# Two transformer blocks on one core: attention heads laid out as 96 rows, another input queue, shared norm banks, block-wise evacuation, another order at the end

## The chip, the core and the metric

The kernel runs on one core of a Trainium2 chip. TensorE (PE) multiplies matrices into PSUM banks, VectorE (DVE), ScalarE (ACT) and GpSimd (POOL) do the element-wise work, and transfers are started from a queue of an engine, most of them from SyncE (SP). The metric is the device time of one execution in microseconds (us), lower is better. It is given as the median of several executions; the profile comes from one more.

## What is computed

256 tokens of width 1024 go through two blocks. The parts that the change touches, from the reference:

```python
def first_block(...):
    xn = rmsnorm(x, norm_mix_g[l])
    proj = jnp.einsum('bsd,de->bse', xn, w_in[l])
    q_lat, kv_lat, k_rope, dq, dk, dv, gate_pre = jnp.split(proj, split_idx, axis=-1)
    q = jnp.einsum('bsr,re->bse', rmsnorm(q_lat, mla_q_norm_g[l]), mla_w_uq[l])
    q_nope, q_pe = q[..., :MLA_NOPE_DIM], apply_rope(q[..., MLA_NOPE_DIM:], ...)   # 64 and 32 of 96
    ...
    q_mla = jnp.concatenate([q_nope, q_pe], axis=-1)
    k_mla = jnp.concatenate([k_nope, jnp.broadcast_to(k_pe, (B, S, MLA_HEADS, MLA_ROPE_DIM))], axis=-1)
    o_mla = causal_attention(q_mla, k_mla, v_mla)                                  # 8 heads
    o_diff = rmsnorm(o1 - lam * o2, diff_subln_g[l]) * (1.0 - lambda_init)         # 4 heads, two maps each
    merged = g_mla * (o_mla @ w_branch_mla[l]) + g_diff * (o_diff @ w_branch_diff[l])
    x = x + jnp.einsum('bsd,de->bse', merged, w_out[l])
    hn = rmsnorm(x, norm_ffn_g[l])
    x = x + (silu(hn @ w_ffn_gate[l]) * (hn @ w_ffn_up[l])) @ w_ffn_down[l]

def second_block(...):      # after a norm of its own
    hx = modulate(rmsnorm_2(x, norm1_g[layer]), sh1, sc1)
    x = x + g1 * (jnp.concatenate([pool_x, attn_x], axis=-1) @ w_out[layer])
    h2 = modulate(rmsnorm_2(x, norm2_g[layer]), sh2, sc2)
    x = x + g2 * peer(h2, ...)        # scores over 128 x 128 experts, then u and v of 16384 x 1024
    return rmsnorm_2(x, final_g)
```

## The kernel before

All of it is one launch on one core. Activations lie transposed (features on the 128 partitions, the 256 tokens along the free axis). Weights are f32 and streamed: `Weights` (L138) loads 128x2048 pieces (`raw`, three buffers) by SP's queue, and splits each 128x1024 half into a rounded high part `whi` by ACT (L133) and a rest `wlo` by DVE (L130), three buffers of each. `mm3` (L167) makes one product out of three matmuls, high x high (L171), low x high (L172) and high x low (L173), so each step of a layer needs whi, wlo and the input's halves. `lin_t` (L175) computes output blocks of 128 features, two of them (`grp=2`) in one PSUM bank, and then calls an evacuation function. PSUM has eight banks: tags a, b, c and d, two of each.

The order on every engine is made by a scheduler from the program's order, its dependences and hints (`tc.issue_after` puts work behind a given instruction); no order is written out by hand.

Stages, in the order of time: the input xT is loaded (L339) and split to xh and xl (`split_x`), POOL squares it (L359) and PE sums the squares with a column of ones (L253). Then come the input projection, the latent projections, the rotations (`rope`, L439), the attention with latent heads, that with differential heads, the gates, the branch products wbm and wbd, wo, the feed-forward, the second block with its own attention and wo2, the search of experts, and the expert products over u and v (v: L1091).

- Latent heads: queries and keys are kept as `qn` and `kn` (two heads of 64 rows on one 128-row tile) and `qp` (four heads of 32 rows) with one shared rotary key `kp`. `soft` (L501) makes the scores of two heads with two matmuls each, one over the 64 rows and one over the 32, adds the mask by a third (L502), takes the row extreme by DVE (L504), the exponential by ACT, and transposes by PE (L513). `pv` (L520) multiplies with the values.
- Differential heads use the same `soft` with one matmul of 64 rows per map. Then `od` is normalised (four nt's, POOL's power, L573), transposed (L576) and split to `odh` by ACT (L579) and `odl` by DVE (L580). These feed wbd; `omh` and `oml` of the latent heads feed wbm.
- Norms: `SumSq` adds up squares over feature blocks and sums over partitions with PE into two PSUM banks, one for each half of the tokens. `rsqrt_cols` (L208) writes one column at a time (nt, by DVE), then POOL raises to the power -0.5 (ny, L219), and PE spreads it over rows (L267).
- wo's evacuation `put_x1` (L612) and wo2's `put_x3` (L819) take two output blocks at once.
- The end: two blocks of 128 experts are done per accumulator, in the order of the four accumulators `acc` (two token halves by two column halves). Then DVE multiplies with the gate (L1131), adds x (L1132), ACT squares (L1133), DVE multiplies with the gain (L1134), and after the factor from POOL ACT scales one half (L1138) and DVE the other (L1139).

Of the kernel before, what the change touches and what calls it, by code (L numbers as in the profile page):

```python
# [63 lines left out]
def block_kernel(ctx: ExitStack, tc: tile.TileContext, a: dict, out: bass.AP, dbg=None):  # L64
# [74 lines left out]
    class Weights:  # L139
# [68 lines left out]
    def rsqrt_cols(vs, scale, nm="n", eps=None):  # L208

        n = len(vs)  # L210
        y = small.tile([P, n], F32, tag=f"{nm}y{n}", name="ny")
        t = small.tile([P, n], F32, tag=f"{nm}t{n}", name="nt")
        for i, v in enumerate(vs):
            c = slice(i, i + 1)
            if eps is None:
                nc.vector.tensor_scalar(t[:, c], v, scale, EPS, op0=OP.mult, op1=OP.add)
            else:
                nc.vector.scalar_tensor_tensor(t[:, c], v, scale, eps, op0=OP.mult, op1=OP.add)
# [3 lines left out]
    class SumSq:  # L222
# [3 lines left out]
        def __init__(self, K, ps_fn, tail=2, held=False):  # L226
            self.held = [] if held else None
            self.K, self.k, self.ps, self.head = K, 0, [ps_fn() for _ in range(2)], K - tail
            self.first = True
            if self.head > 0:  # L230
                self.acc = adap.tile([P, S], F32, tag="sqa", bufs=2, name="sqa")

        def add(self, src, scale=None, sq=None):
# [11 lines left out]
            if k >= self.head - 1:  # L245
                if self.held is None:
                    self.total(sq, k)
                else:
                    self.held.append((sq, k))

        def total(self, sq, k):
            for tt in range(2):
                nc.tensor.matmul(self.ps[tt][:, 0:1], sq[:, tt * P:(tt + 1) * P], ones[:, 0:1],  # L253
                                 start=self.first, stop=(k == self.K - 1))
            self.first = False

        def done(self):
            for h in self.held or ():
                self.total(*h)
            return [p_[:, 0:1] for p_ in self.ps]  # L260
# [89 lines left out]
    subg = b1a.tile([P, 1], F32, name="subg")  # L350
    nc.scalar.activation(subg, col("sub"), AF.Copy, scale=1.0 - LAMBDA_INIT)
    load_x(0)
# [56 lines left out]
    nc.vector.tensor_copy(posf, posi)  # L409
    identb = b1a.tile([P, P], BF16, name="identb")  # L410
    nc.vector.tensor_copy(identb, ident)
    maskb = b1a.tile([P, P], BF16, name="maskb")
    nc.vector.tensor_copy(maskb, cs1[:, CB["mask"] - NCB])

    def rope_tables(inv, nm):
# [3 lines left out]
        for shift, kind in ((0.0, "s"), (math.pi / 2, "c")):  # L419
            ki = b1s.tile([P, S], I32, tag="ki", bufs=2, name="ki")  # L420
            nc.vector.tensor_scalar(ki, ang, 1.0 / TWO_PI, shift / TWO_PI, op0=OP.mult, op1=OP.add)
            kf = b1s.tile([P, S], F32, tag="kf", bufs=2, name="kf")
# [16 lines left out]
    def rope(x_, n, rt, cc, ss):  # L439
        for j in range(0, n, 2):  # L440
# [6 lines left out]
            nc.vector.tensor_tensor(x_[:, j:j + m], x_[:, j:j + m], t1[:, :m], op=OP.add)  # L447
# [79 lines left out]
    for qb in range(2):  # L527
        o = ps_d()
        z = small.tile([P, 8], F32, tag="az", name="az")
        for h0 in range(4):  # L530
            b0, r0 = 64 * (h0 % 2), 32 * h0
# [20 lines left out]
    for qb in range(2):  # L552
# [19 lines left out]
        yd = rsqrt_cols([ss[:, h:h + 1] for h in range(4)], 1.0 / 128, "d")  # L572
# [36 lines left out]
    ss1 = SumSq(KD, ps_d, held=True)  # L609
# [12 lines left out]
    b2 = pool(st3, "b2")  # L622
    st3c = ExitStack()
# [5 lines left out]
    hs = scaled_split(x1, KD, lambda k: col("ffn", k), acts, "act")  # L629
# [25 lines left out]
    def modulated(src, rb, gs, sh, hi, lo):  # L655
        for k in range(KD):
            t = adap.tile([P, S], F32, tag="mdt", bufs=4, name="mdt")
# [41 lines left out]
    with tc.high_priority():  # L699
# [8 lines left out]
        for i in range(2):  # L708
            c = slice(i, i + 1)
            nc.vector.scalar_tensor_tensor(t[:, c], sg[i], yf[:, c], yf[:, c], op0=OP.mult, op1=OP.mult)  # L710
        y3 = rsqrt_cols([t[:, 0:1], t[:, 1:2]], 1.0 / D, "m")
# [102 lines left out]
    ss3 = SumSq(KD, ps_d, held=True)  # L814

    def put_x3(j, n, ps):
# [454 lines left out]
```

## Time and profile before

| what | us |
|---|---|
| median of three executions | 1413.62 (1412.87 to 1416.95) |
| the profiled execution | 1420.62 |
| its span (first to last instruction on record) | 1418.8 |
| busy in the span: PE, DVE, ACT, POOL | 1375.2, 1013.1, 704.9, 23.8 |

The mean granted clock of PE over the span was 0.984 of full speed. A busy engine is one that has an instruction in flight; for PE, matmuls overlap in the array, so a row's duration is longer than the distance to the next start, and it is the distance that counts. A gap in brackets is idle time of the engine ahead of that row, with what ended it.

### The profile page before, as it was taken

The page shows a single profiled execution, that of the slowest core. Times are in us where ns is not written, and L with a number is a line of the kernel's source. Part 1 is how long each engine was busy: PE and PEld are TensorE (multiplying, and loading weights), DVE is VectorE, ACT ScalarE, POOL GpSimd, SP SyncE. Part 2 cuts the span into 40 slices and gives each one's busy share as a digit, 9 for nine tenths or more (in the row PEclk, how much of TensorE's full clock was granted, in tenths as well). Part 3 has the DMA queues.
Part 4 walks back from the last instruction along what each step waited for, and adds up shares of the span by engine and source line. Part 5 has one row for each costly group of instructions (what it writes and reads, how often), then busy time and mean ns, then how long its engine had stood idle before and what let it go on. Part 6 is the DMA issues. An engine that isn't in the chain of part 4 may idle for free.

```text
span 1418.8 us, 24208 instructions
## 1 busy us (share of the span) xinstructions
PE 1375.2 (97%) x9776; PEld 1270.8 (90%) x9776; DVE 1013.1 (71%) x1749; ACT 704.9 (50%) x1030; POOL 23.8 (2%) x25
## 2 busy tenths in 40 slices
PE   7999999999999999899999999998999999999997
PEld 6967998999999888899999999998888888888885
DVE  6774777998888646699984489876536555566775
ACT  4443654454546555545454456554344454444443
POOL 1000000000000001000000000000000000000000
PEclk9998999999999999999999999999899999999999
DMA  6452456777795632444555578889975555588762
GB/s 239 154 196 82 141 169 234 269 279 267 262 328 191 218 125 72 152 170 158 187 198 180 178 257 311 296 296 321 340 287 197 190 197 199 198 300 289 262 233 86
DMA packets 88448, 308.86 MB, mean 218 GB/s; under 512 B 6416, under 2 KB 39824, under 8 KB 61200
## 3 DMA queue, kind: packets, MB, share of 16 engines
q1 hardware_dynamic: 78544, 279.26, 57.0%
q10 hardware_dynamic: 9792, 28.05, 5.0%
q8 instruction: 76, 1.25, 0.3%
q14 instruction: 36, 0.29, 0.1%
HBM read 281.08 MB, written 26.21 MB: 217 GB/s over the span
## 4 chain that ended last, share of the span: by engine, by line
PE 88%; DVE 5%; DMA 4%; issue 1%; ACT 1%; POOL 0%; SPq 0%; ACTq 0%; POOLq 0%; DVEq 0%
PE acc L1091 24%; PE psa L173 9%; PE psa L171 9%; PE psa L172 9%; PE psc L173 8%; PE psc L171 8%; PE psc L172 8%; DMA aw<-in_ada 2%; PE psb L501 2%; DVE wlo L130 2%; PE psd L1012 1%; PE psb L1012 1%; DMA gh<-ggd 1%; PE psd L771 1%; PE psb L759 1%
## 5 line engine op out<-in xcount | busy, mean ns | idle before, releaser
L133 ACT ACTIVATE whi<-raw 128x1024 fp32r<-128x1024 f32 (+1 forms) x426 | 448.0, 1053 | 502.7 <-PE psa L172 181.6
L130 DVE TENSOR_TENSOR wlo<-raw,whi 128x1024 fp32r<-128x1024 f32 (+1 forms) x426 | 517.4, 1217 | 240.6 <-ACT whi L133 236.9
L171 PE MATMUL psc<-h2h,whi 128*128 128x256 f32 x1024 | 294.3, 288 | 6.4 <-ACT whi L133 6.4
L173 PE MATMUL psc<-h2h,wlo 128*128 128x256 f32 x1024 | 293.8, 288 | 4.2 <-DVE wlo L130 4.2
L172 PE MATMUL psc<-h2l,whi 128*128 128x256 f32 x1024 | 292.7, 286 | 0.0
L171 PEld LDWEIGHTS psc<-h2h,whi 128*128 128x128 f32 x1024 | 199.8, 195 | 7.0 <-ACT whi L133 7.0
L173 PEld LDWEIGHTS psc<-h2h,wlo 128*128 128x128 f32 x1024 | 199.5, 195 | 4.9 <-DVE wlo L130 4.9
L172 PEld LDWEIGHTS psc<-h2l,whi 128*128 128x128 f32 x1024 | 199.8, 195 | 0.0
L1091 PE MATMUL acc<-wlo,wgh 128*128 128x512 f32 x512 | 160.2, 393 | 0.0
L1091 PE MATMUL acc<-whi,wgl 128*128 128x512 f32 x512 | 158.7, 390 | 0.0
L1091 PE MATMUL acc<-whi,wgh 128*128 128x512 f32 x512 | 138.5, 389 | 0.0
L1091 PEld LDWEIGHTS acc<-whi,wgl 128*128 128x128 f32 x512 | 96.1, 188 | 20.2
L1091 PEld LDWEIGHTS acc<-whi,wgh 128*128 128x128 f32 x512 | 96.0, 188 | 20.1
L1091 PEld LDWEIGHTS acc<-wlo,wgh 128*128 128x128 f32 x512 | 94.6, 188 | 19.7
L171 PE MATMUL psa<-acth,whi 128*128 128x256 f32 x352 | 99.9, 284 | 2.0 <-DVE ft L638 1.2
L173 PE MATMUL psa<-acth,wlo 128*128 128x256 f32 x352 | 99.9, 284 | 1.9 <-DVE wlo L130 1.9
L172 PE MATMUL psa<-actl,whi 128*128 128x256 f32 x352 | 99.8, 284 | 0.2 <-DVE actl L293 0.2
L171 PE MATMUL psa<-xh,whi 128*128 128x256 f32 x240 | 71.1, 296 | 8.0 <-ACT whi L133 8.0
L173 PE MATMUL psa<-xh,wlo 128*128 128x256 f32 x240 | 70.4, 293 | 2.6 <-DVE wlo L130 2.6
L172 PE MATMUL psa<-xl,whi 128*128 128x256 f32 x240 | 71.0, 296 | 0.0
L316 DVE SCALAR_TENSOR_TENSOR jk<-aw,row_c 128x1024 bf16<-128x1024 f32 x48 | 58.6, 1220 | 14.8 <-DMA aw<-in_ada 14.4
L171 PEld LDWEIGHTS psa<-acth,whi 128*128 128x128 f32 x352 | 66.9, 190 | 2.6 <-ACT whi L133 1.4
(415 smaller groups left out, 2462.6 us busy)
## 6 DMA issues: line engine op xcount, KB each, us to landing
raw<-in_uT SPq DMA_DIRECT2D x64, 1024.0 KB, 4.9
raw<-in_v SPq DMA_DIRECT2D x64, 1024.0 KB, 4.9
aw<-in_ada SPq DMA_DIRECT2D x48, 512.0 KB, 5.8
raw<-in_wgu SPq DMA_DIRECT2D x22, 1024.0 KB, 4.9
ggd<-gs ACTq DMA_DIRECT2D x32, 512.0 KB, 4.5
gh<-ggd SPq DMA_DIRECT2D x8, 2048.0 KB, 14.3
raw<-in_wA SPq DMA_DIRECT2D x14, 1024.0 KB, 5.0
raw<-in_wdn SPq DMA_DIRECT2D x11, 1024.0 KB, 7.2
```

The costliest lines, as they stand in the source:

```text
L130: e.tensor_tensor(dst, src, hi.bitcast(F32), op=OP.subtract)
L133: nc.scalar.activation(dst_h, src, AF.Copy)
L171: nc.tensor.matmul(ps, wh, xs[0][:, k], start=(k == 0), stop=False)
L172: nc.tensor.matmul(ps, wh, xs[1][:, k], start=False, stop=False)
L173: last_mm[0] = nc.tensor.matmul(ps, wl, xs[0][:, k], start=False, stop=(k == K - 1))
L316: nc.vector.scalar_tensor_tensor(jk, aw, 1.0, c_, op0=OP.mult, op1=OP.mult, accum_out=dst[:, t:t + 1])
L501: nc.tensor.matmul(s[:, i], q_[:, qb * P:(qb + 1) * P], k_[:, :n], start=(j == 0), stop=False)
L759: nc.tensor.matmul(s, q2[x_][hd, hp, qs_], kall[y_][hd, hp], start=(i == 0), stop=(i == 2))
L771: nc.tensor.matmul(o[:, h * 64:(h + 1) * 64], pts[:, kb * P:(kb + 1) * P], v2[:, kb, h * 64:(h + 1) * 64], start=(kb == 0), stop=(kb == 3))
L1012: nc.tensor.matmul(ps[:, t4 * P:(t4 + 1) * P], o1[:, 2 * g4 + t4 // 2, :, t4 % 2], og[:, c, 2 * g4 + t4 // 2, :, t4 % 2], start=(c == 1), ...
L1091: r = nc.tensor.matmul(acc[tt][n], x_, w_[:, n * 512:(n + 1) * 512], start=st, stop=sp)
```

## The change

1. `qh` and `kh` hold each head as 96 rows (64 without rotation, 32 with it). `soft` gets one matmul per head. The evacuations of wuq and wuk write even and odd heads separately (`nope`), the last step of the rotation of qp writes four pieces, and ACT copies the rotated shared key to all eight heads.
2. xT comes in four transfers on ACT's queue, and SP's first weight piece is cut into 512 + 512 + 1024 columns. The squares of xT move from POOL to ACT. Three small casts move behind the scores' first hints.
3. `SumSq` sums both token halves in one bank, all of it at the end (`done`); `rsqrt_cols` takes all columns in one instruction. For x1 and x3 one tail term replaces two.
4. wo and wo2 are evacuated one block of 128 features at a time, and x1's halves `hs` are made there instead of behind the layer.
5. The last three expert blocks instead of two are done per accumulator. One of DVE's instructions at the end goes, and ACT and DVE share the scaling differently.

```diff
+                    ends = (0, 512, 1024, w) if self.fine and c == 0 else (0, w)
+                    for o, e in zip(ends, ends[1:]):
                         last_load[0] = nc.sync.dma_start(self.raw[:, o:e], self.src[:, c + o:c + e])
...
-        for i, v in enumerate(vs):
-            c = slice(i, i + 1)
...
-                nc.vector.tensor_scalar(t[:, c], v, scale, EPS, op0=OP.mult, op1=OP.add)
+            nc.vector.tensor_scalar(t, v, scale, EPS, op0=OP.mult, op1=OP.add)
...
+        def done(self):
             for tt in range(2):
+                for i, sq in enumerate(self.sqs):
+                    nc.tensor.matmul(self.ps[:, tt:tt + 1], sq[:, tt * P:(tt + 1) * P], ones[:, 0:1],
+                                     start=(i == 0), stop=(i == len(self.sqs) - 1))
+            return self.ps[:, 0:2]
...
-        k = slice(4 * i, 4 * i + 4)
-        nc.sync.dma_start(xT[:, k], a["xT"].rearrange("p (k t) -> p k t", k=KD)[:, k])
+        k = slice(2 * i, 2 * i + 2)
+        nc.scalar.dma_start(xT[:, k], a["xT"].rearrange("p (k t) -> p k t", k=KD)[:, k])
...
-        nc.gpsimd.tensor_tensor(sq0[:, k], xT[:, k], xT[:, k], op=OP.mult)
+        nc.scalar.activation(sq0[:, k], xT[:, k], AF.Square)
...
+                for r, o in outs(j, m):
+                    nc.vector.tensor_tensor(o, x_[r, j:j + m], t1[r, :m], op=OP.add)
...
+    nc.scalar.activation(kh[64:96], kp[64:96].to_broadcast([32, 8, S]), AF.Copy)
+    def nope(dst, j, n, ps, rb):
+        for e in range(2):
+            r = slice(64 * e, 64 * e + 64)
+            nc.vector.tensor_tensor(dst[0:64].rearrange("p (j e) t -> p e j t", e=2)[:, e, j:j + n], ps[r],
+                                    rb[r][:, None, :].to_broadcast([64, n, S]), op=OP.mult)
...
-            ptss = soft([[(qn[b0:b0 + 64, h // 2], kn[b0:b0 + 64, h // 2]),
-                          (qp[r0:r0 + 32, h // 4], kp[r0:r0 + 32, 0])] for h in pair], qb,
-                        [z[:, h:h + 1] for h in pair])
+            ptss = soft([[(qh[:, h], kh[:, h])] for h in pair], qb, [z[:, h:h + 1] for h in pair])
...
     def put_x1(j, n, ps):
-        nc.vector.tensor_tensor(x1[:, j:j + n], ps, xT[:, j:j + n], op=OP.add)
-        for i in range(n):
-            ss1.add(x1[:, j + i])
-    lin_t(a["wo"], 8, KD, (mh, ml), put_x1)
+        nc.vector.tensor_tensor(x1[:, j], ps[:, 0], xT[:, j], op=OP.add)
+        nc.scalar.activation(hs[0][:, j], x1[:, j], AF.Copy, scale=col("ffn", j))
+        nc.vector.scalar_tensor_tensor(hs[1][:, j], x1[:, j], col("ffn", j), hs[0][:, j].bitcast(F32),
+                                       op0=OP.mult, op1=OP.subtract)
+        ss1.add(x1[:, j])
+    lin_t(a["wo"], 8, KD, (mh, ml), put_x1, grp=1)
...
-    lin_t(a["wo2"], 8, KD, (cath, catl), put_x3)
+    lin_t(a["wo2"], 8, KD, (cath, catl), put_x3, grp=1)
...
-                        for i in range(2):
-                            r = block(i, tt, (n,))
+                        for b in range(NE - 3, NE):
+                            r = block(b, tt, (n,))
...
-            nc.vector.tensor_tensor(xn[:, h_], o[:, h_], fg[:, h_], op=OP.mult)
+            if tt == 0 or n == 0:
+                nc.vector.tensor_tensor(xn[:, h_], o[:, h_], fg[:, h_], op=OP.mult)
```

The scheduler gives another order in several places. PE in the latent-head scores with 256 columns, before (psb is the scores' bank, maskb and identb add the mask):

```order
L173 MATMUL psa<-xh,wlo 128x256
L501 MATMUL psb<-knope,qnope 128x256
L501 MATMUL psb<-kp,qp 128x256
L502 LDWEIGHTS identb
L502 MATMUL psb<-maskb,identb 128x128
L501 MATMUL psb<-knope,qnope 128x256
L501 MATMUL psb<-kp,qp 128x256
```

and after (the transposes of probabilities, psc<-cst,prob, now stand between the scores):

```order
L517 MATMUL psc<-cst,prob 128x128
L505 MATMUL psb<-kh,qh 128x256
L517 MATMUL psc<-cst,prob 128x128
L506 LDWEIGHTS identb
L506 MATMUL psb<-maskb,identb 128x128
L505 MATMUL psb<-kh,qh 128x256
```

Each head has one score matmul less, and transposes of earlier probabilities moved in between. PE at the second transposes of od, before:

```order
L173 MATMUL psa<-omh,wlo 128x256
L576 MATMUL psc<-cst,od 128x128 x4
L171 MATMUL psa<-omh,whi 128x256
L172 MATMUL psa<-oml,whi 128x256
L173 MATMUL psa<-omh,wlo 128x256
```

and after:

```order
L171 MATMUL psa<-omh,wlo 128x256
L577 MATMUL psc<-cst,od 128x128 x4
L169 MATMUL psa<-odh,whi 128x256 x2
L170 MATMUL psa<-odl,whi 128x256
L171 MATMUL psa<-odh,wlo 128x256
```

The transposes moved behind the omh products, to stand directly ahead of the products of odh and odl that they feed. DVE at the norm of x3, before (xT<-psa,mod,xT is x3's block, kall holds its halves, nt goes to POOL):

```order
L819 SCALAR_TENSOR_TENSOR xT<-psa,mod,xT 128x256 x2
L130 TENSOR_TENSOR wlo<-raw,whi 128x1024
L827 SCALAR_TENSOR_TENSOR kall_4843<-xT,gs_4033,kall_4842 128x256 x2
L216 TENSOR_SCALAR nt<-psd 128x1
L130 TENSOR_TENSOR wlo<-raw,whi 128x1024
L216 TENSOR_SCALAR nt<-psd 128x1
```

and after:

```order
L820 SCALAR_TENSOR_TENSOR xT<-psa,mod,xT 128x256
L130 TENSOR_TENSOR wlo<-raw,whi 128x1024
L824 SCALAR_TENSOR_TENSOR kall_4832<-xT,gs_4024,kall_4831 128x256
L212 TENSOR_SCALAR nt<-psd 128x2
L130 TENSOR_TENSOR wlo<-raw,whi 128x1024 x2
```

The two nt's with a weight split between them became one, and x3's blocks are evacuated one at a time.

## Rows read from the trace of the kernel before

**Rows 1.** The page: busy time and share of each engine; the chain by engine.

```profile
PE 1375.2 (97%) x9776; PEld 1270.8 (90%) x9776; DVE 1013.1 (71%) x1749; ACT 704.9 (50%) x1030; POOL 23.8 (2%) x25
...
PE 88%; DVE 5%; DMA 4%; issue 1%; ACT 1%; POOL 0%; SPq 0%; ACTq 0%; POOLq 0%; DVEq 0%
```

**Rows 2.** PE's waits: what waited, for what; us, times, longest.

```profile
PE psa L171 <- ACT whi L133: 8.0, 1, 8.0
...
PE psa L171 <- DVE pq L887: 2.8, 1, 2.8
...
PE psd L267 <- POOL ny L219: 1.7, 1, 1.7
...
PE psa L171 <- DVE ft L638: 1.2, 1, 1.2
```

**Rows 3.** Stretches: us, busy time (instructions) per engine, granted clock, DMA share, GB/s.

```profile
4.00:8.00 4.00, 0.02 (x1) 0.02 (x1) 1.75 (x2) 2.29 (x6) 1.89 (x1) 1.00 1.01 371
70.00:80.00 10.00, 10.00 (x41) 6.30 (x40) 10.00 (x16) 7.78 (x8) 0.00 (x0) 1.00 0.98 382
82.00:86.00 4.00, 4.00 (x11) 2.42 (x10) 3.29 (x7) 0.81 (x4) 0.00 (x0) 0.57 0.01 2
106.00:116.00 10.00, 10.00 (x35) 7.06 (x34) 2.08 (x3) 1.82 (x5) 0.00 (x0) 0.50 0.00 0
120.00:140.00 20.00, 20.00 (x148) 17.19 (x148) 9.46 (x16) 7.93 (x24) 0.00 (x0) 1.00 0.23 86
1000.00:1020.00 20.00, 16.61 (x117) 16.20 (x116) 13.77 (x19) 6.96 (x9) 0.00 (x0) 0.85 1.11 341
```

**Rows 4.** PE in time, latent-head scores: start, us, line, out<-in, count.

```profile
90.86 0.48 PE L501 MATMUL psb<-kp,qp 32*128 32x128 f32 x2
91.28 0.23 PE L502 MATMUL psb<-maskb,identb 128*128 128x128 bf16 x1
...
102.75 0.70 PE L501 MATMUL psb<-knope,qnope 64*128 64x256 f32 x2
103.37 0.69 PE L501 MATMUL psb<-kp,qp 32*128 32x256 f32 x2
104.00 0.23 PE L502 MATMUL psb<-maskb,identb 128*128 128x128 bf16 x1
```

**Rows 5.** DVE in time, evacuation of the no-rope query block; gap before it in brackets.

```profile
62.23 0.69 DVE L477 TENSOR_TENSOR qnope<-psa,rbq 128x512 f32<-128x512 f32 x1 [1.03 <-PE psa L173]
```

**Rows 6.** PE and DVE in time at the second transposes of od.

```profile
189.09 0.60 PE L576 MATMUL psc<-cst,od 128*128 128x128 f32 x4
...
190.44 0.75 DVE L580 SCALAR_TENSOR_TENSOR odl<-psc,subg,odh 128x512 fp32r<-128x512 f32 x1 [0.35 <-ACT odh L579]
```

**Rows 7.** Start, in time: ACT, DVE, PE, each with its gap.

```profile
16.33 1.06 ACT L133 ACTIVATE whi<-raw 128x1024 fp32r<-128x1024 f32 x1 [5.33 <-DMA raw<-in_wA]
...
6.25 4.50 DVE L344 SCALAR_TENSOR_TENSOR xl<-xT,cols,xh 128x256 fp32r<-128x256 f32 x4 [6.25 <-ACT xh L343]
...
11.88 1.66 DVE L344 SCALAR_TENSOR_TENSOR xl<-xT,cols,xh 128x256 fp32r<-128x256 f32 x4
...
11.41 0.58 PE L173 MATMUL psa<-xh,wlo 128*128 128x256 f32 x1 [2.63 <-DVE wlo L130]
```

**Rows 8.** PE and DVE in time at the norm of x3.

```profile
580.43 1.03 PE L253 MATMUL psd<-cst,sq 128*128 128x1 f32 x8
...
581.28 0.16 DVE L216 TENSOR_SCALAR nt<-psd 128x1 f32<-128x1 f32 x1 [3.53 <-PE psd L253]
...
582.48 0.15 DVE L216 TENSOR_SCALAR nt<-psd 128x1 f32<-128x1 f32 x1
```

**Rows 9.** The end in time: last block's low half, last matmul, last scaling.

```profile
1402.33 1.23 DVE L130 TENSOR_TENSOR wlo<-raw,whi 128x1024 fp32r<-128x1024 f32 x1 [1.43 <-ACT whi L133]
...
1408.97 0.39 PE L1091 MATMUL acc<-whi,wgl 128*128 128x512 f32 x1
...
1414.35 0.72 ACT L1138 ACTIVATE fin<-fin,ny 128x512 f32<-128x512 f32 x1 [0.86 <-POOL ny L219]
```

More of the change, by code (lines that the diff above doesn't have):

```diff
@@ L222, in block_kernel, with __init__ @@
     class SumSq:
[L226 to L229, printed above, removed]
+        def __init__(self, K, ps_fn, tail=2):
+            self.K, self.k, self.ps, self.head = K, 0, ps_fn(), K - tail
+            self.sqs = []
             if self.head > 0:
@@ L245, in add @@
             if k >= self.head - 1:
[L246 to L251, printed above, removed]
-            for tt in range(2):
[L253 to L260, printed above, removed]
+                self.sqs.append(sq)
+        def done(self):
+            for tt in range(2):
+                for i, sq in enumerate(self.sqs):
+                    nc.tensor.matmul(self.ps[:, tt:tt + 1], sq[:, tt * P:(tt + 1) * P], ones[:, 0:1],
+                                     start=(i == 0), stop=(i == len(self.sqs) - 1))
+            return self.ps[:, 0:2]
     last_bc = [None]
@@ L350, in block_kernel @@
     subg = b1a.tile([P, 1], F32, name="subg")
+    for i in range(4):
+        load_x(i)
     nc.scalar.activation(subg, col("sub"), AF.Copy, scale=1.0 - LAMBDA_INIT)
-    load_x(0)
     split_x(0)
@@ L408, in block_kernel @@
     posf = b1s.tile([P, S], F32, name="posf")
-    nc.vector.tensor_copy(posf, posi)
     identb = b1a.tile([P, P], BF16, name="identb")
-    nc.vector.tensor_copy(identb, ident)
     maskb = b1a.tile([P, P], BF16, name="maskb")
-    nc.vector.tensor_copy(maskb, cs1[:, CB["mask"] - NCB])
+    with tc.issue_after(put[0].ins):
+        nc.vector.tensor_copy(posf, posi)
+        nc.vector.tensor_copy(identb, ident)
+        nc.vector.tensor_copy(maskb, cs1[:, CB["mask"] - NCB])
     def rope_tables(inv, nm):
@@ L437, in block_kernel, with rope @@
         s_d, c_d = rope_tables(col("inv1"), "d")
-    def rope(x_, n, rt, cc, ss):
+    def rope(x_, n, rt, cc, ss, outs=None):
         for j in range(0, n, 2):
@@ L571, in block_kernel @@
             nc.scalar.activation(t2[:, h], od[:, h], AF.Square, accum_out=ss[:, h:h + 1])
-        yd = rsqrt_cols([ss[:, h:h + 1] for h in range(4)], 1.0 / 128, "d")
+        yd = rsqrt_cols(ss, 1.0 / 128, "d")
         nc.vector.tensor_tensor(od, od, hb(yd, 4, P), op=OP.mult)
@@ L813, in block_kernel, with put_x3 @@
     z3 = [x.rearrange("p a (b t) -> p (a b) t", b=2)[:, :, :S + 2] for x in kz]
[L814 to L829 removed]
+    ss3 = SumSq(KD, ps_d, 1)
+    def put_x3(k, n, ps):
+        nc.vector.scalar_tensor_tensor(x3[:, k], ps[:, 0], mod[:, 16 + k:17 + k], xb[:, k], op0=OP.mult, op1=OP.add)
+        g = gs2[:, k:k + 1]
+        zh, zl = (z[:, k, :S] for z in z3)
+        nc.scalar.activation(zh, x3[:, k], AF.Copy, scale=g)
+        nc.vector.scalar_tensor_tensor(zl, x3[:, k], g, zh.bitcast(F32), op0=OP.mult, op1=OP.subtract)
+        ss3.add(x3[:, k])
+    lin_t(a["wo2"], 8, KD, (cath, catl), put_x3, grp=1)
     tap("x3", x3)
@@ L1082, in v_pass, with block @@
             end = jj + 2 == NE
-            hls = [w((j + i) * KD, KD) for i in range(2)]
-            def block(i, tt, ns):
-                hi, lo = hls[i]
-                first, last = jj + i == 0, jj + i == NE - 1
-                th, tl = wh[:, i, tt * P:(tt + 1) * P], wl[:, i, tt * P:(tt + 1) * P]
+            for i in range(2):
+                last3[jj + i] = *w((j + i) * KD, KD), wh[:, i], wl[:, i]
+            def block(b, tt, ns):
+                hi, lo, th, tl = last3[b]
+                first, last = b == 0, b == NE - 1
+                th, tl = th[:, tt * P:(tt + 1) * P], tl[:, tt * P:(tt + 1) * P]
                 for x_, w_, st, sp in ((th, hi, first, False), (th, lo, False, False), (tl, hi, False, last)):
@@ L1094, in v_pass @@
             if not end:
-                for i, tt in itertools.product(range(2), range(2)):
-                    block(i, tt, range(2))
+                for i, tt in itertools.product(range(1 if jj + 4 == NE else 2), range(2)):
+                    block(jj + i, tt, range(2))
             else:
```

75 lines of the change are left out of this document (34 added, 41 removed).

## The prediction

> **What bounds the kernel now.** I read the page's busy line and its chain first: TensorE (PE) is busy 97% of the span, VectorE (DVE) 71%, ScalarE (ACT) 50%, and the chain that ended last runs through PE for 88% of its length [rows 1]. So a microsecond is won in three ways only: fewer or shorter matmuls, fewer waits of PE, or a tail that is shorter after the last matmul. Then the list of PE's waits: the longest are the start (8.0 us until the first weight block is split [rows 2], 2.63 more for its low half [rows 7]), then 2.8 us for pq, 1.7 us for the norm factor ny of x3, 1.2 us for ft [rows 2]. All waits and the tail make up the 3% that PE idles. Last the table of stretches with the granted clock. A busy PE isn't a fast PE: in the latent-head attention 82 to 86 us ran at 0.57 and 106 to 116 us at 0.50 (the lower level, 1.2 GHz), though PE is busy throughout; the differential attention at 120 to 140 us, the same work with one score matmul per head instead of two, ran at 1.00 [rows 3].
>
> The profiled execution took 1420.62 us, the median of the runs is 1413.62; the sum is made against the first, and 7.0 us are taken off at the end.
>
> **Part 1, heads as 96 rows.** Removed are 16 score matmuls with 32 rows, 8 of 128 columns and 8 of 256. Each is two passes in the trace. From start to start the pair takes 0.42 us with 128 columns (90.86 to 91.28) and 0.63 with 256 (103.37 to 104.00), as the 64-row pair of 256 columns just before it (0.62) [rows 4]. The remaining matmul gets 96 rows for 64; since 32 and 64 rows cost the same, I take 96 to cost the same. At full clock: 8 x 0.42 + 8 x 0.625 = **-8.4 us**, on PE, in a stretch where PE is busy 20.0 of 20 us, so all on the path.
>
> The clock is the second half. 4.0 us at 0.57 and 10.3 at 0.50 lost 1.7 and 5.2 us against full clock [rows 3] (4.0 x 0.43, and 10.3 x 0.50 with the 0.3 us behind 116). PE came to 106 us through groups of two heads' scores with 9 to 13 wide products between one group and the next; the new order has groups of four heads with 36 to 48 between them, so fewer of the narrow rows in one stretch, which is nearer to the differential attention and its 1.00. So I take the second loss as gone, **-5.2**, and the first as staying (0), because DVE is the busier there. Bounds: -6.9, or -1.0 (the low stretch stays, and its two removed pairs give 1.05 more than at full clock, half speed being twice 0.63).
>
> What it adds: the 64-row evacuations of the two no-rope projections need eight instructions of 512 columns instead of four (0.69 us each [rows 5]), and the last step of qp's rotation writes four 32-row pieces instead of one, so 4 x 0.64 + 3 x 0.64 = about 4.5 us of DVE work, between 60 and 82 us. DVE is busy 10.00 of 10 us from 70 to 80 [rows 3]; of the 4.5 about 3.4 can fall into the four gaps that DVE has between 60 and 69 us (the longest, 1.03, is shown [rows 5]) if they come in time. From PE's side the scores are reached as qh gets ready, a wait of 0 to 3 us; I take 0, as rotations of dq and dk, needed 40 us later, can go behind. The copy of the shared rotary key to eight heads is one ACT instruction of 2048 columns; ACT is busy 50% and nothing waits for it.
>
> The new order also closes a gap: the second block's transposes of od stand right before the odh products, where before some 70 products of omh stood between. The chain behind the transposes is visible now: they start at 189.09, odl ends at 191.19, 2.1 us later [rows 6]. Nothing covers it any more: **+2.1** (1.4, if products with odh alone go first, to 2.8, if the extra split that stands ahead of odl on DVE is late). Part 1: -8.4 - 5.2 + 2.1 = -11.5.
>
> **Part 2, input by ScalarE's queue.** Now PE's first product waits 8.0 us [rows 2], its third until 11.41: DVE's first four xl took 4.50 us from 6.25, its other four 1.66 [rows 7], and POOL squared the same rows beside the first (1.89 us busy from 4 to 8 [rows 3]). With the squares on ACT, that slowdown should go: DVE reaches wlo about 2.8 us earlier. But the transfers aren't fewer, the DMA engines are at 1.01 of their time from 4 to 8 us [rows 3], the next weight block lands only at 16.33 [rows 7], and two squares of about 1.05 us (what ACT takes for 128x1024) now stand between ACT's splits. PE works on its first 26 products until 16.7 now; I place their end at 13 to 14, and then PE waits for the block that lands at 16.3, with the sums of squares (2 us) pulled into that wait. So **-2.0** (0 to -3.5).
>
> The Trainium skill ("Trainium Kernel Development and Optimization", Key Constraints) says that transfers issued by SP, ACT and POOL run on the same 16 DMA engines, and that several issuers save issue time alone. The trace shows the engines full from 4 to 8 us, which agrees; if that were all, the start would give back about 0.5 us and the sum below would be 1.5 us smaller.
>
> **Part 3, both sums in one bank.** Of one sum of squares 38 products remain from 42 in all (x1 and x3 sum one tail term fewer), two passes each. Eight passes in a row are on record with 1.03 us, the end of the last included [rows 8]: **-0.8**. The factor instructions halve: at x3 the second nt starts 1.20 us after the first because a weight split stands between [rows 8]; as one instruction it is done 1.2 us earlier. PE waits 1.7 us there for ny, but 2.8 us later for pq [rows 2], which part of the gain runs into: **-1.0** (0 to -2). For x1 the same split stands between, PE's wait for ft is 1.2 us [rows 2].
>
> **Part 4, block by block.** wo's and wo2's results are evacuated per 256 columns and x1's halves hs are made inside the layer. Same number of columns, 8 instructions for 4; the last block's actl stands behind a weight split of 1.22 us, so it is ready about 1.8 us after PE wants it; against that stand ft's 1.2 [rows 2] and three waits of 0.2 to 0.6 on these values now, in all 1.0. Parts 3 and 4 at x1: **-0.5** (-2 to +2).
>
> **Part 5, the end.** The last matmul starts at 1408.97 and the last scaling at 1414.35 [rows 9]. Three blocks instead of two per accumulator put 0.7 us more between the accumulators, so DVE's four evacuations start earlier against the end, and one product leaves the chain: -1.7. But the last group's first nine products need wlo of the last block, which is split at 1402.33 to 1403.56 now [rows 9], after whi, which starts as PE releases its buffer; PE gets there about 1.2 us sooner. **-0.5** (-1.7 to +0.8).
>
> **Sum.** -11.5 - 2.0 - 0.8 - 1.0 - 0.5 - 0.5 = -16.3: profiled 1404.3, median **1397**. With every bound at its better end (1.7 of clock, 0.7 at odh, 1.5 at the start, 1.0, 1.5 and 1.2 behind) 7.6 less, 1389.
>
> **Rivals.**
> (a) The clock falls as before. For it: PE was busy 10.00 of 10 us in the low stretch [rows 3], so no idle time need come with it, and the new order keeps 16 scores in that place. Then 4.2 us of the 5.2 are not won: 1401.5.
> (b) The DVE chain binds in the attention. For it: 10.00 of 10 busy [rows 3], and 4.5 us more work. If the whole 4.5 fall on PE, odh costs 2.8, x1 +2 and the clock stays low: 1397.3 + 4.5 + 0.7 + 2.5 + (0 to 4.2) = 1405 to 1409.
> (c) The 32-row products already run beside the 64-row ones. Against it: a 32-row pair takes its full 0.42 or 0.63 behind a 64-row pair, as long as the 64-row pair itself [rows 4]. Then the 8.4 us would not be won, 1405.7. By the Trainium skill ("TensorE: Matmul & The Clock Gate", Packing small matmuls) products in distinct row groups of the array run concurrently, which would speak against this change; the trace shows no overlap.
> (d) Slower: the new DVE work makes PE wait in every head, and PE runs as in 1000 to 1020 us, where it stood for 3.4 us of 20 and was granted 0.85, together some 6.4 us lost per 20 [rows 3]. It decides from 16.3 / 6.4 = 2.5 such stretches; over the four of 60 to 140 us the kernel ends at 1397.3 + 25.6 = 1423. Against it: the slack that the scheduler finds in 120 to 140, where DVE is at 9.46 of 20.
>
> **Chances.** Forecast 0.50; (a) 0.23; (b) 0.16; (c) 0.04; (d) 0.07. 0.3% is 4.2 us, about what a measurement of this kernel can tell from no change, so faster means under 1409.4: forecast, (a), (c) and half of (b), 0.85; the other half within, 0.08; slower 0.07. The range takes the best bounds and (b) up to 1408: 1389 to 1408.
>
> **What would show it.** In the table of stretches the clock between 80 and 120 us is 0.95 or more, and differential attention begins 10 to 14 us sooner; a new PE wait of about 2 us on odl stands in the list of waits; the first products are continuous from before 10 us, with a wait for raw at 14 to 16; at x3 one nt, and PE's wait for ny under 1 us; the last matmul stands about 8 us ahead of the span's end, against 9.4. Wrong is the forecast if the score stretch shows PE waits for DVE that add up to over 5 us, or a lower clock where it was 1.00.

## The result, and the profile after

| | before | changed |
|---|---|---|
| median of four executions, us | 1415.28 (1412.87 to 1417.83) | 1399.06 (1397.90 to 1403.02) |
| ratio, 95% interval | | 0.989 (0.9861 to 0.9919) |
| profiled execution / its span, us | 1420.62 / 1418.8 | 1397.90 / 1396.1 |

The kernel is faster by 16.2 us, forecast were 16.6 (1413.62 to 1397). The stages below show that most terms behind this sum were not of the forecast size, so that the total came out right is luck in part. The page of the changed kernel, busy time:

```profile
PE 1357.0 (97%) x9736; PEld 1262.0 (90%) x9736; DVE 1014.2 (73%) x1746; ACT 709.3 (51%) x1034; POOL 20.2 (1%) x23
```

PE is busy 18.2 us less than in [rows 1] and idles 39.1 us instead of 43.6. PE's waits in the changed kernel (us in total, times, longest):

```profile
PE psa L169 <- ACT whi L133: 6.8, 2, 6.5
...
PE psa L169 <- DVE pq L885: 3.4, 1, 3.4
PE psd L255 <- POOL ny L215: 1.8, 1, 1.8
...
PE psa L169 <- ACT odh L580: 1.2, 1, 1.2
...
PE psa L170 <- DVE odl L581: 0.8, 1, 0.8
PE acc L1091 <- DVE wlo L130: 0.8, 1, 0.8
```

Against [rows 2]: ft is gone, the start is shorter, but the waits for pq and ny are longer, not shorter, and odh and odl are new. The stretches with the latent heads (columns as in [rows 3]):

```profile
80.00:100.00 20.00, 20.00 (x135) 17.69 (x134) 20.00 (x33) 12.70 (x29) 0.00 (x0) 1.00 0.55 186
100.00:120.00 20.00, 20.00 (x159) 18.38 (x157) 16.28 (x26) 10.72 (x33) 0.00 (x0) 1.00 0.47 168
```

The clock is at 1.00 throughout. DVE is busy 20.00 of 20 us from 80 to 100 and PE waits for nothing there: products of dv and of the gates stand between the scores.

To see where the time went, every kernel's trace was cut at the same matmuls, each the first of its kind: of the latent keys (psa<-kvh), of wo (mh), of the feed-forward's second layer (hidh), of the second block (h1h), of the expert scores (psc<-h2h), of the expert outputs (acc), and the last matmul. Every column is the distance from the one before, in us of the profiled execution:

| kernel | start | attention | x1, FFN in | FFN out | to x3, experts' search | u | v | tail | span |
|---|---|---|---|---|---|---|---|---|---|
| before | 66.27 | 144.85 | 159.00 | 90.53 | 175.89 | 420.10 | 352.33 | 9.87 | 1418.8 |
| before again (e3) | 64.96 | 143.15 | 158.45 | 89.58 | 174.28 | 420.02 | 352.34 | 9.88 | 1412.7 |
| changed | 65.52 | 128.95 | 154.10 | 88.79 | 176.31 | 420.19 | 353.48 | 8.75 | 1396.1 |
| e1 part 1 alone | 66.31 | 129.21 | 158.50 | 89.29 | 170.49 | 417.66 | 352.33 | 9.87 | 1393.7 |
| e2 parts 2 to 5 | 66.71 | 154.71 | 156.10 | 90.24 | 175.72 | 418.43 | 353.48 | 8.54 | 1423.9 |
| e4 changed + zero scores | 64.39 | 136.26 | 155.96 | 90.68 | 176.16 | 420.24 | 353.60 | 8.75 | 1406.0 |
| h2 parts 1, 2 | 67.19 | 131.49 | 158.77 | 89.98 | 174.29 | 420.13 | 352.34 | 10.02 | 1404.2 |
| h3 parts 1, 3 | 65.67 | 129.82 | 162.04 | 88.69 | 174.57 | 420.15 | 352.74 | 9.88 | 1403.6 |
| h4 parts 1, 4 | 66.19 | 131.09 | 163.31 | 88.92 | 175.50 | 420.22 | 352.33 | 9.86 | 1407.4 |
| h5 parts 1, 5 | 66.28 | 130.32 | 157.49 | 88.77 | 172.10 | 418.21 | 353.49 | 8.43 | 1395.1 |
| f1 part 1, cT later | 66.26 | 129.29 | 158.51 | 89.21 | 170.49 | 418.06 | 352.34 | 10.51 | 1394.7 |
| f2 parts 1, 4, cT later | 65.64 | 130.33 | 156.17 | 88.72 | 172.14 | 419.97 | 352.34 | 10.49 | 1395.8 |
| f3 changed, not part 3 | 63.86 | 130.28 | 158.86 | 88.82 | 170.59 | 419.90 | 353.45 | 8.56 | 1394.3 |
| f4 the same, cT later | 65.01 | 130.02 | 156.28 | 88.73 | 170.59 | 419.26 | 353.50 | 8.55 | 1391.9 |

The attention gave 14 to 16 us against the two traces of before, the x1 stage 4 to 5, the rest +2 us against the first trace and -2 against the second.

These are single traces, and part of the differences between them is the clock. At x3, PE's wait for ny (1.67 to 1.78 us) is followed by a stretch of 3.4 us at 0.50 (the lower level, 1.2 GHz) in all fourteen traces. A wait for pq of 2.8 us or more comes with a second one (3.4 or 6.8 us) in all eight traces that have it; the waits of 0.4 to 0.6 us in the other six come with none. Each begins within 1.3 us of the wait's end. A stretch of 3.4 us at 0.50 loses 1.7 us, about as much as the wait for ny itself. In the attention, h2, h4 and h5 have one behind the new waits for odh and odl (at 184 to 187 us); the other seven traces with part 1 and these waits have none.

### The profile page after: what moved, and what is told of

The parts are those of the page before. It is cut to its first block, busy times and chain, and to the rows that moved or that the text cites. A ratio compares the mean times of both kernels' runs of the same rounds, so it can differ in the third digit from the quotient of the medians.

```text
span 1396.1 us, 24126 instructions
## 1 busy us (share of the span) xinstructions
PE 1357.0 (97%) x9736; PEld 1262.0 (90%) x9736; DVE 1014.2 (73%) x1746; ACT 709.3 (51%) x1034; POOL 20.2 (1%) x23
## 4 chain that ended last, share of the span: by engine, by line
PE 92%; DVE 4%; DMA 2%; ACT 1%; issue 1%; POOL 0%; ACTq 0%; SPq 0%; POOLq 0%; DVEq 0%
PE acc L1091 24%; PE psa L171 10%; PE psa L170 10%; PE psa L169 10%; PE psc L171 9%; PE psc L169 9%; PE psc L170 8%; DVE wlo L130 1%; PE psd L1010 1%; PE psb L1010 1%; DMA gh<-ggd 1%; PE psd L774 1%; DMA raw<-in_wA 1%; PE psb L505 1%; PE psb L762 1%; PE psd L524 1%
## 5 line engine op out<-in xcount | busy, mean ns | idle before, releaser
L171 PEld LDWEIGHTS psa<-acth,wlo 128*128 128x128 f32 x352 | 67.6, 192 | 0.8 <-DVE wlo L130 0.8
```

Of the source, the lines that this page charges most:

```text
L171: last_mm[0] = nc.tensor.matmul(ps, wl, xs[0][:, k], start=False, stop=(k == K - 1))
```

## The experiments

Medians and ratios, each against the kernel before on the same chip. e1 to e4, h2 to h5 and f1 to f4 are three groups, in which the kernel before had medians of 1416.96, 1418.77 and 1414.33 us, so kernels of different groups are compared by their ratios (0.001 is 1.4 us):

| run | median, us | ratio, 95% interval |
|---|---|---|
| e1 part 1 alone | 1396.62 | 0.9863 (0.9835 to 0.9891) |
| e2 parts 2 to 5 | 1413.82 | 0.9986 (0.9966 to 1.0007) |
| e3 before again | 1415.82 | 0.9990 (0.9972 to 1.0009) |
| e4 changed + zero scores | 1411.83 | 0.9973 (0.9948 to 0.9997) |
| h2 parts 1, 2 | 1402.13 | 0.9881 (0.9855 to 0.9906) |
| h3 parts 1, 3 | 1404.46 | 0.9901 (0.9876 to 0.9925) |
| h4 parts 1, 4 | 1407.92 | 0.9931 (0.9905 to 0.9958) |
| h5 parts 1, 5 | 1396.99 | 0.9853 (0.9829 to 0.9877) |
| f1 part 1, cT later | 1396.21 | 0.9868 (0.9840 to 0.9896) |
| f2 parts 1, 4, cT later | 1398.94 | 0.9886 (0.9857 to 0.9914) |
| f3 changed, not part 3 | 1396.51 | 0.9872 (0.9843 to 0.9901) |
| f4 the same, cT later | 1396.07 | 0.9865 (0.9836 to 0.9893) |

**e1, part 1 alone**, on the kernel before; the edit is part 1's piece of the diff, mdt's buffers move to a pool that opens later, and two small tiles of the rotation tables keep one buffer instead of two, to make room:

```diff
+    mdp = pool(st3, "mdp", 4)
...
-            t = adap.tile([P, S], F32, tag="mdt", bufs=4, name="mdt")
+            t = mdp.tile([P, S], F32, tag="mdt", name="mdt")
```

> The kernel before with part 1 alone (heads as 96 rows; the pool of mdt is moved to make room). Theory of the prediction: 8.4 us of score matmuls and 5.2 us of lowered clock go, about 2 us of wait for odh and odl come, so 10 to 13 us faster than before (ratio 0.991 to 0.993). Rival 'the clock fell only in some executions of before': 5 to 8 us faster (0.9945 to 0.9965), since the 5.2 us were a matter of the profiled run. Rival 'the new order of the loads is what helped': under 4 us faster here.

Measured: 20.3 us faster, more than any theory had and as fast as the whole change. Of the 25.1 us between the traces, 15.6 are in the attention; 5.4 and 2.4 are in the x3 and u stages, where part 1 has no instruction, though the moved buffers of mdt are used at x3. There the scheduler now puts one weight split of DVE ahead of pq instead of two, PE's wait is 0.42 us instead of 2.82, and the clock stood at 0.50 for 3.4 us instead of three times 3.4. At the change from u to v the clock fell less, to 0.96 over 80 us instead of 0.89 in the changed kernel; 0.07 x 80 is 5.6 us, of which the stage shows 2.5. PE idles about 11 of these 80 us in both; what sets the rest is not shown.

**e2, all but part 1.** The four pieces of part 1 are taken back in the changed kernel.

> The changed kernel with part 1 undone, so parts 2 to 5 alone. Theory of the prediction: 5 us faster than before (ratio 0.9965); by the trace of the changed kernel, whose start, x1 stage and feed-forward gave 1, 4 and 2 us and whose x3 stage and end gave nothing, 6 to 7 us (0.9955). Rival 'most of the gain is the heads': within 2 us of before.

Measured: 3.1 us, and "same" isn't ruled out. Its profiled execution, the longest of its 13 (1407.62 to 1425.99), shows the clock in the latent heads:

```profile
80.00:100.00 20.00, 20.00 (x83) 14.62 (x83) 14.47 (x23) 8.22 (x22) 0.00 (x0) 0.85 0.51 191
100.00:120.00 20.00, 20.00 (x66) 12.37 (x65) 6.89 (x11) 4.64 (x16) 0.00 (x0) 0.59 0.00 0
120.00:140.00 20.00, 20.00 (x105) 16.84 (x105) 8.46 (x13) 7.95 (x22) 0.00 (x0) 0.71 0.22 80
```

20 x (0.15 + 0.41 + 0.29) = 17 us lost in 60, where the first trace of before lost 7. PE was busy all the time; in the 20 us ahead of the fall (at 93.9 us) it had no wait.

**e3, the kernel before again.**

> The kernel before once more, for a second trace of it. If the fall of the clock at 82 to 86 and 106 to 116 us belongs to the kernel, it is there again, and DVE waits again about 3 us for aw at 246 us; the time is that of before (ratio 0.998 to 1.002). If they were chance, the clock in 100 to 120 us is 1.00 and the trace is some 5 us shorter.

Measured: the fall at 100 us was there again, the one at 82 wasn't, and DVE waited 1.86 us for aw instead of 3.26.

```profile
80.00:100.00 20.00, 20.00 (x99) 14.28 (x98) 15.73 (x25) 9.36 (x26) 0.00 (x0) 1.00 0.43 159
100.00:120.00 20.00, 20.00 (x87) 13.68 (x87) 6.46 (x11) 6.24 (x20) 0.00 (x0) 0.74 0.22 79
```

So the fall belongs to the kernel, its length varies. The kernel before ran 29 times beside these four runs: 1409.53 to 1422.88 us, granted clock over the span 0.989 in the fastest and 0.982 in the slowest.

**e4, 16 zero scores more.** In the changed kernel, each head gets a second matmul of 32 rows against zeros:

```diff
+    qz = b1a.tile([96, S], F32, name="qz")
+    nc.gpsimd.memset(qz, 0.0)
...
-            ptss = soft([[(qh[:, h], kh[:, h])] for h in pair], qb, [z[:, h:h + 1] for h in pair])
+            ptss = soft([[(qh[:, h], kh[:, h]), (qz[64:96], kh[64:96, h])] for h in pair], qb, [z[:, h:h + 1] for h in pair])
```

> The changed kernel with 16 more score matmuls of 32 rows, which add zeros (a tile of zeros against the rotary rows of kh), in the places where the kernel before had them. Theory 'each 32-row matmul costs as much as a 64-row one': 8.4 us slower than the changed kernel, 13 us if the clock falls with them. Rival 'row groups run side by side': no slower than the changed kernel.

Measured: 11.7 us slower than the changed kernel by the ratios. Each pair of 128 columns takes its full 0.41 to 0.42 us, as in [rows 4]; PE in time:

```profile
87.82 0.48 PE L507 MATMUL psb<-kh,qz 32*128 32x128 f32 x2
88.23 0.23 PE L508 MATMUL psb<-maskb,identb 128*128 128x128 bf16 x1
```

In its trace, whose clock stayed at 1.00 there, the attention is 7.3 us longer than in the changed kernel; that one has 2.1 us of waits for odh and odl that e4, with its own order, hasn't, so the scores alone cost about 9.4. Counted from start to start, the zero matmuls take 8.3 us, and the 96-row ones beside them 1.4 more than in the changed kernel. Its twelve times spread from 1404.81 to 1423.74 at clocks over the span from 0.989 to 0.980. That would fit a fall in the latent heads in part of the executions, but no trace of a slower one is on record, so it is not shown. The zeros lie in rows 64 to 95, which the 96-row matmul ahead of them uses too, so e4 can't tell whether matmuls in distinct rows run side by side; it shows that an extra narrow matmul costs its full time here.

**h2 to h5: part 1 and one other part each.** The edits are those of the diff.

> Parts 1 and 2 (heads, input by ScalarE's queue), against part 1 alone at 1396.6 us. Theory of the prediction: 2 us faster, 1394.6. Rival 'the start only moves its wait': PE begins 1.5 us sooner and waits for the second weight block instead, 1396 to 1397, and the latent projections begin within 0.5 us of part 1 alone.

Measured: not faster (by the ratios 2.5 us slower than e1, the intervals overlap). PE starts at 6.60 instead of 8.24 and reaches the latent keys at 67.19 instead of 66.31, so the theory failed, and the rival's 0.5 us was missed too. Of the 10.5 us between the traces only 0.9 are in the start; 2.3 are in the attention, 3.8 at x3 and 2.5 in u.

> Parts 1 and 3 (heads, both sums in one bank, one nt), against part 1 alone at 1396.6 us. Theory of the prediction: 1.5 to 2 us faster, PE's wait for ny at x3 under 1 us. Rival 'GpSimd's power waits out the weight split that DVE starts beside it': ny takes 1.8 us instead of 0.7 at x3, PE waits for it 1.7 us or more as before, and only the 0.8 us of shorter sums stay.

Measured: 5.4 us slower than e1 by the ratios, the intervals just overlap. The rival holds for ny; that the time would be 3.5 us longer at x1 and 4.1 at x3 neither theory said. POOL at x3 in h3, and then in e1, where two nt's stand with a weight split between:

```profile
565.34 1.74 POOL L217 TENSOR_TENSOR ny<-nt,mhalf 128x2 f32<-128x2 f32 x1 [40.53 <-DVE nt L214]
```

```profile
563.86 0.71 POOL L219 TENSOR_TENSOR ny<-nt,mhalf 128x2 f32<-128x2 f32 x1 [41.92 <-DVE nt L216]
```

As one nt is ready, DVE goes straight on to the split that used to stand between, and POOL takes 1.74 us instead of 0.71 beside it. At x1 PE waits 3.42 us for wlo behind a wait of DVE of 3.51 us for aw, and the clock stood at 0.50 for 6.8 us (e1: 3.4).

> Parts 1 and 4 (heads, wo and wo2 evacuated by the block), against part 1 alone at 1396.6 us. Theory of the prediction: no change within 2 us. Rival, from the trace of the changed kernel: the four waits of PE around x1 (4.4 us in all before) shrink to under 1 us, 1393 to 1394.

Measured: 9.6 us slower than e1 by the ratios, intervals apart. Neither theory held. The x1 stage is 4.8 us longer: DVE stood 4.49 us for a load of aw, with the weight splits behind it in its queue, and the clock stood at 0.50 twice for 3.4 us there (once in e1), 1.7 us more lost. The x3 stage is another 5.0 longer, with two splits ahead of pq. DVE, then PE:

```profile
232.58 1.23 DVE L316 SCALAR_TENSOR_TENSOR jk<-aw,row_c 128x1024 bf16<-128x1024 f32 x1 [4.49 <-DMA aw<-in_ada]
...
235.01 0.39 PE L173 MATMUL psa<-acth,wlo 128*128 128x256 f32 x1 [2.00 <-DVE wlo L130]
...
243.18 0.55 PE L171 MATMUL psa<-acth,whi 128*128 128x256 f32 x1 [3.26 <-DVE ft L652]
```

> Parts 1 and 5 (heads, other order at the end), against part 1 alone at 1396.6 us. Theory of the prediction: 0.5 us faster: a tail about 1 to 1.7 us shorter after the last matmul, less a wait for the last low half ahead of it. Rival, from the trace of the changed kernel: both are the same size (1.15 us), 1396 to 1397; PE waits 0.8 us on wlo in the last accumulators.

Measured: the rival. v is 1.16 us longer, the tail 1.44 shorter; the ratios are 0.001 apart, which is nothing.

**f1 to f4.** The load of the context, cT, goes on ScalarE's queue at x1 and takes 9.5 us to land in h4, but 4.8 in the changed kernel, where DVE doesn't wait for aw. The edit of f1 (on e1), f2 (on h4) and f4 (on f3):

```diff
-    nc.scalar.dma_start(cT, a["ctxT"].rearrange("p (k t) -> p k t", k=KD))
...
+    with tc.issue_after(silus[4].ins):
+        nc.scalar.dma_start(cT, a["ctxT"].rearrange("p (k t) -> p k t", k=KD))
```

f3 is the changed kernel with part 3's pieces taken back. Each of these runs was profiled once, and a moved load also changes the order.

> Part 1 alone with one more edit: the 1 MB load of the context cT on ScalarE's queue is issued behind the fifth silu of the feed-forward instead of at x1. Theory 'cT's load delays the load of aw, for which DVE waits, and PE behind it': DVE's two waits for aw at 229 and 239 us (1.83 and 1.22) shrink under 0.5, PE's 1.0 us there goes, 1395 to 1396. Rival 'aw is late by itself': no wait moves, 1396.6. The order at the norm of x3 is that of part 1 alone, so first h2h to pq should keep a wait under 1 us.

Measured: DVE's waits for aw are gone, but PE's wait of 1.03 us at 237 us stays, now as before for whi; no gain. In e1 the late load cost nothing that PE saw.

> Parts 1 and 4 with the load of cT issued behind the fifth silu. Without that edit they took 1407.9 us, DVE waited 4.49 and 1.54 us for aw behind cT, and PE 2.00 and 3.26 us behind DVE. Theory 'cT's load delays aw': those waits go, 5 us less. The edit also puts the order at x3 back (one weight split ahead of pq instead of two): by the theory 'the order of the weight splits at x3 sets the wait for pq' another 4 to 6 us less, so 1397 to 1399. If only one of the two holds, 1402 to 1404; if neither, 1408.

Measured: 1398.94, in the range of both theories together; by the ratios 6.4 us less than h4, with overlapping intervals. In the traces the x1 stage is 7.1 us shorter (PE's waits there are about 4.5 us less, and no stretch at 0.50 is left of two), the x3 stage 3.4, and there PE's wait for pq fell from 2.8 to 0.5. DVE's first wait for aw in f2:

```profile
227.64 1.23 DVE L316 SCALAR_TENSOR_TENSOR jk<-aw,row_c 128x1024 bf16<-128x1024 f32 x1 [0.95 <-DMA aw<-in_ada]
```

> The changed kernel with part 3 alone undone (two banks, one nt per column). The sums gave back 0.8 us of matmuls, but with them GpSimd's power ran beside a weight split (1.79 us instead of 0.71), and two splits stand ahead of pq. Theory 'part 3 costs more through the order at x3 than it saves': x3 stage 4 to 6 us shorter than in the changed kernel, wait for pq under 1 us, 1393 to 1397 if the x1 stage keeps its order. Rival 'part 3 helps as forecast': 1 to 2 us slower than the changed kernel, 1400 to 1401.

Measured: 1396.51, in the range of the first theory, though its condition, the x1 stage as it was, failed; by the ratios 2.5 us less than the changed kernel, intervals overlapping, so against the rival and not proof of the other. The x3 stage is 5.7 us shorter than in the changed kernel, x1 4.8 longer. PE's waits in f3:

```profile
PE psa L169 <- DVE ft L652: 2.1, 1, 2.1
PE psd L265 <- POOL ny L217: 1.7, 1, 1.7
```

The wait for pq is 0.57, and that for ny is the same 1.7 with one nt or two.

> The changed kernel without part 3 and with the load of cT behind the fifth silu. If both theories hold (aw late through cT, and the order at x3), this beats both kernels: no wait of DVE for aw over 1 us between 210 and 260 us, a short x3 stage, 1390 to 1394. If cT is no matter, the same as without part 3 alone.

Measured: 1396.07 (1393.43 to 1397.48), the shortest trace of all; but its ratio's interval overlaps that of the changed kernel, f3 and e1, so a version that beats the changed one is indicated and not shown. The forecast of both theories, 1390 to 1394, was missed, and by the ratios f4 is only 1 us less than f3, which is what the other one said (cT no matter). Of the signs, the short x3 stage came, as in f3; x1 is 2.6 us shorter than in f3; but DVE still waits 1.23 us for aw at 227 us.

## Why the prediction was right, and where its steps were not

**The baseline.** Three executions had a median of 1413.62, 29 later ones 1416.96. The profiled one was 7.0 us above the first; I took these off the result as well. But three executions were too few, and the 7.0 us belong to the kernel before: the changed kernel's profiled execution stands 1.2 us below its median. How much of the variation of before is its clock in the latent heads is not shown; its two traces differ by 6.1 us, of which 1.7 are in the attention. The profiled sum was 1404.3 and came out as 1397.9, the median was 1397 and came out as 1399.1; two errors met.

**Part 1** was the gain, and larger: forecast -11.5, measured -15.9 in the attention against the first trace of before, -14.2 against the second. The step that failed is "since 32 and 64 rows cost the same, I take 96 to cost the same". The 96 rows cost less. PE in the changed kernel, beside [rows 4]:

```profile
86.50 0.39 PE L505 MATMUL psb<-kh,qh 96*128 96x128 f32 x2
86.72 0.22 PE L506 MATMUL psb<-maskb,identb 128*128 128x128 bf16 x1
...
97.09 0.65 PE L505 MATMUL psb<-kh,qh 96*128 96x256 f32 x2
97.58 0.22 PE L506 MATMUL psb<-maskb,identb 128*128 128x128 bf16 x1
```

From start to start the two passes of a matmul with 96 rows take 0.22 us with 128 columns (0.28 right behind a mask) and 0.43 to 0.49 with 256, where those with 64 or 32 rows take 0.42 and 0.63. The records of the weight loads (PEld) show a difference that goes with it; before, then changed:

```profile
90.86 0.29 PEld L501 LDWEIGHTS psb<-kp,qp 32*128 32x128 f32 x2
```

```profile
86.39 0.30 PEld L505 LDWEIGHTS psb<-kh,qh 96*128 96x128 f32 x2
```

The narrow load starts with its matmul, at 90.86; the 96-row one at 86.39, 0.11 us ahead of its matmul and beside the one before. Summed over all scores of the latent heads, start to start and at full clock, 16.0 us became 5.8: -10.2 for the forecast -8.4, and the mask matmuls behind them took 0.6 less. The clock came back in full, 6.8 us in the first trace of before (1.7 and 5.1) and 5.1 in the second. The new wait was priced right: 1.22 us for odh and 0.84 for odl where 2.1 were forecast. -10.2 - 0.6 - 6.8 + 2.1 = -15.5 of the -15.9.

DVE's 4.5 us more work cost PE nothing in the changed kernel, as taken; in six other kernels with part 1 PE waits 0.3 to 1.0 us for kh. Rival (b) found DVE full and no wait; (a) and (d) did not come about in the changed kernel; e2 shows what (a) costs at its worst. Rival (c) falls with [rows 4]. But its words "the trace shows no overlap" hold for the 32-row pairs alone: in the trace of before four passes with 64 rows, two heads' scores, took the time of two:

```profile
72.46 0.49 PE L501 MATMUL psb<-knope,qnope 64*128 64x128 f32 x4
```

Two of them start 0.006 us apart. By the masks that follow they are heads 0 and 1, in rows 0 to 63 and 64 to 127; the rows are not on record, so that is inferred. Putting the narrow matmuls of heads in different rows side by side is thus another way to part of this gain, which no run tested.

Why the clock fell is open. It fell in the latent heads in all three traces with 64-row and 32-row scores (before, e3, e2) and in none of the ten with 96 rows alone, but not in e4's trace either, and the differential heads keep their 64-row scores at 1.00, but for the fall of e2 that reaches into them.

**Part 2** was mis-sized: -2.0 forecast. Over all traces the start takes 63.9 to 67.2 us in the six with part 2 (mean 65.4) and 65.0 to 66.3 in the eight without (mean 66.0). PE starts 1.5 us sooner; the step that failed was "PE waits for the block that lands at 16.3". There is no such wait: but for 0.67 us, products and the sums of squares fill the time to 17.6, and PE stands 0.28 us for wlo at 18.3. What the prediction had no term for is the clock. ACT and PE in the changed kernel, and a stretch of it (columns as in [rows 3]):

```profile
15.96 2.00 ACT L133 ACTIVATE whi<-raw 128x1024 fp32r<-128x1024 f32 x2 [3.67 <-DMA raw<-in_wA]
...
15.86 1.84 PE L246 MATMUL psd<-cst,gates 128*128 128x1 f32 x16
```

```profile
16.00:20.00 4.00, 3.72 (x27) 3.52 (x26) 2.80 (x4) 3.02 (x3) 0.37 (x1) 0.79 0.71 299
```

From 18.3 to 21.7 the clock was at 0.50, products stood 0.21 us apart instead of 0.12, and 1.7 us were lost. In f3, with the same part 2 and no fall there, the start takes 63.86, 2.4 us less than before. The second block is split from 15.96 as it was from 16.33 [rows 7]. In the mean part 2 gave 0.5 us. The sum that the prediction gave beside the Trainium skill's rule on the 16 DMA engines ("Trainium Kernel Development and Optimization", Key Constraints) had 0.5 us for the start.

**Part 3**: the shorter sums came as forecast (76 passes instead of 84, 1.0 us between e1 and the changed kernel). The main step failed: "as one instruction it is done 1.2 us earlier" holds for nt and not for ny. PE's wait is 1.78 against 1.67, and pq's 3.44 against 2.82. DVE and POOL in the changed kernel, beside [rows 8]:

```profile
557.89 0.16 DVE L212 TENSOR_SCALAR nt<-psd 128x2 f32<-128x2 f32 x1 [3.62 <-PE psd L246]
558.13 2.36 DVE L130 TENSOR_TENSOR wlo<-raw,whi 128x1024 fp32r<-128x1024 f32 x2
...
558.13 1.79 POOL L215 TENSOR_TENSOR ny<-nt,mhalf 128x2 f32<-128x2 f32 x1 [42.17 <-DVE nt L212]
```

POOL's power took 0.71 us in the kernels with two nt's here and 1.74 to 1.79 in those with one. The Trainium skill ("SBUF — State Buffer", SBUF: two separate sides) has the rule: DVE and GpSimd share a pair of ports under an exclusive lock, a DVE instruction with two inputs in SBUF takes it against a GpSimd instruction that reads SBUF, and whichever starts first holds it to its end. The trace agrees: the split reads raw and whi, and 1.79 - 0.71 = 1.08 us is most of its 1.22. By that rule, with a split right behind nt, next to nothing of the gain at ny was to be had; it spoke against this part, and I did not weigh it. Besides, in all four kernels with one nt two weight splits stand between ny's use and pq; with two nt's there are two in before, e3, h2 and h4, and one in e1, h5 and f1 to f4, so that the one nt causes it is not shown. f3 gets 5.7 us back in that stage: 3.0 are waits (ny 1.78 and pq 3.44 against 1.67 and 0.57), and about 3.4 the clock, which stood at 0.50 for 3.4 us three times in that stage of the changed kernel (at 530, 561 and 571 us) and once in f3, less what f3's longer sums cost. The changed kernel and f3:

```profile
550.00:600.00 50.00, 44.78 (x351) 44.39 (x350) 38.85 (x145) 24.93 (x45) 1.79 (x1) 0.93 0.41 148
```

```profile
550.00:600.00 50.00, 47.76 (x389) 47.38 (x389) 42.19 (x159) 27.66 (x49) 0.71 (x1) 0.97 0.46 168
```

**Parts 3 and 4 at x1** were taken as -0.5, with bounds -2 to +2; measured -4.9 together against before (-4.4 against e1), and +3.5 and +4.8 apart against e1. Two steps failed. The 1.8 us that the sum set for actl did not come: PE's waits in that stage fell from 4.4 us in all to 0.9. And PE's wait for ft was read as one on DVE, but DVE itself had waited 3.26 us for a load of aw in the kernel before, a row that the prediction didn't look up:

```profile
246.48 1.23 DVE L316 SCALAR_TENSOR_TENSOR jk<-aw,row_c 128x1024 bf16<-128x1024 f32 x1 [3.26 <-DMA aw<-in_ada]
```

In h4 most of it is the load of cT beside it: with that load later, in f2, DVE waits 0.95 us instead of 4.49. Why the changed kernel's cT lands in 4.8 us is not settled.

**Part 5**: -0.5 forecast, 0.0 measured: the tail is 1.1 us shorter, the wait for wlo of the last block and what stands around it cost 1.15.

## What to carry to other kernels

Narrow matmuls can cost PE more than fuller ones: here a pass of 128 columns took 0.21 us with 32 or 64 rows and 0.11 to 0.16 with 96, and a busy PE did not show it. Read the distance from start to start for each shape, and do not carry it from one shape to another. Merging them gave the whole gain here, about two thirds of it from shorter matmuls and the rest from a clock that no longer fell. Where a scheduler sets the order, a part's worth is not a constant: stages that no edit touched moved by 5 us (e1 and h2 differ at x3 alone by 3.8), so forecast the order first and the cost then, and follow a wait to its first cause, which can be a load behind the engine that PE waits for. Before you speed up what feeds a small GpSimd instruction, see what DVE will do beside it.

## What the runs showed of the hardware

- Falls of the clock without any wait of PE: in the latent heads 0.59 over 20 us with PE busy 20.00 (e2). The lower level came in runs of narrow score matmuls (before, e3, e2); with one 96-row matmul a head no profiled execution showed it there.
- Stretches of 3.4 us at 0.50 at a wait of PE: at x3 right behind or at the end of the wait of 1.7 to 1.8 us for ny in all fourteen traces.
- The distance from one matmul pass to the next: 0.20 to 0.21 us (128 columns) and 0.31 to 0.32 (256) with 32 and with 64 rows; 0.11 to 0.16 and 0.22 to 0.27 with 96.
- One GpSimd instruction of two columns took 0.71 or 1.79 us, by which engine started first.
- The 1 MB load of cT on ScalarE's queue, with loads on SP's queue beside it, took from 4.8 us (changed) to 10.2 us (before) to land, and DVE waited up to 4.49 us for the load of aw beside it (h4).
